# Two filter taps per slot until the second pair's keys, and second-layer scores one slot after the first transposes

## The chip, the cores and the metric

The kernel runs on one core of a Trainium2 chip. Its engines run side by side, each through its own list of instructions in order: TensorE (PE, matmuls), VectorE (DVE), ScalarE (ACT), GpSimd (POOL) and SyncE (SP, which issues most DMAs). The metric is the device time of one execution in microseconds.

## The reference

Two layers run over 256 latent tokens, which layer 1 extends by 256 context tokens. Each layer projects the normalised tokens to a convolution branch, queries, keys and values of eight attention heads, and gates; both branches are joined by the gates and projected out, and a gated MLP follows. Cut to what bears on the change:

```python
p = h @ w_in[l]
u = a * jax.nn.sigmoid(g)                  # convolution branch, 512 channels
u = dwconv1d(u, dw, dw_b)                  # 31 taps along the tokens
u = jax.nn.silu(layernorm(u, ln_g, ln_b)) @ w_conv_out
q, k = rope_2d(q, ...), rope_2d(k, ...)
s = concat([s_window + bias, s_context])   # neighbourhood window and all context keys
y_attn = merge_heads(softmax(s) @ v) @ w_na_out
x = x + g1 * ((g_conv * y_conv + g_attn * y_attn) @ w_out)
x = x + g2 * conv_ffn(h2, w_up, dw, dw_b, w_down)
```

All is float32.

## The kernel before, in words

Tokens lie along the free dimension: 512 columns in the first layer (`self.l` or `l` is 0), 256 in the second (`last`), where only the keys and values still have context columns. Weights come as units of 128 x 1024, loaded by SP. Every float32 product is three matmuls (`mm3`, L187 to L189): high part of the weights by high and low part of the tokens, low part of the weights by the high part of the tokens. ACT casts the high part of a unit (L168 or L206); the low part is a subtraction on DVE (L169), or, for some units, a negation on ACT (L207) and an accumulating DMA that POOL issues (L208). The names in a trace are `whi` and `wlo` for these, `h` for the tokens' parts, `raw` for a unit as loaded.

A *group* is eight such products into one PSUM bank, 24 matmuls. After each group of 256 columns, and twice in a group of 512, `slot()` lets every side generator go one step. The side generators spread other work between the groups:

- `conv_run` (the convolution) takes `rate[0]` taps per slot from a list; a tap is one DVE instruction on one of four channel tiles (`cb`, L651; the first of a tile is L649).
- `Attention.run` calls `step()`. Heads go in four pairs. `qk(j)` makes a pair's queries and keys: two groups, rotary products on DVE (L839 to L849), the high part on ACT (L861), the low part on DVE (L862), and a load of the bias on SP (L837). `pair(j)` then puts the pair on `todo`, with the slot at which it came. `issue()` takes it from there: score products on PE (L472, twelve for the latent queries), which fill four PSUM banks (`sc`, `sc`, `pt`, `main`), and the softmax: bias and maximum on DVE (L493), exponential on ACT (L496), reciprocal on DVE (L498), scaling on ACT (L499). The result is `pp`. `turn()` transposes it on PE (L538) into the same four banks and copies these out on ACT (L541, for the context queries L544). `values()` makes the products with the values (L555, L564) into the bank `po`, which ACT and DVE empty (L572, L573).

`self.soft` holds softmaxes that wait to be transposed, `self.pv` transposes that wait for their values, `self.at` the number of the last step that did something. A step issues, in one go, transposes of the last pair, values of the one before it, and scores of the next. While nothing is waiting for its values yet, that is at the first transposes, `alone` makes the first layer issue the transposes by themselves; `late` then has the next scores issued at the next slot.

After the attention and the gates (`gate`, L693 and L696) comes the layer norm of the convolution, again as a side generator: it takes the taps that are left, five or six a slot, sums on PE (L939, L354), spreads the reciprocal root (L369), and writes the result's parts `sh` and `sl` (L950 to L954). Then PE runs the attention's projection (U_NA, on `oh` and `ol`), the convolution's (U_CO, on `sh` and `sl`), where DVE joins the branches (L977, L982 to L985), and the output projection.

A scheduler puts the instructions of this program into a list per engine, by priorities and modelled times; `issue_after` binds some to a place. So an edit of when something is issued can move rows on every engine.

Of the kernel before, what the change touches and what calls it, by code (L numbers as in the profile page):

```python
# [53 lines left out]
def trunk(ctx: ExitStack, tc: tile.TileContext, xt, cvec, crow, wall, wada, params, bias_t, rope_t, out):  # L54
# [13 lines left out]
    def nm(s):  # L68
        uid[0] += 1
        return f"{s}_{uid[0]}"  # L70
# [3 lines left out]
    def psum(tag="main"):  # L74
        return psp.tile([P, 512], F32, tag=tag, bufs=BANKS[tag], name=nm(tag))

    def tmp(w=512):
        return tp.tile([P, w], F32, tag="t", bufs=5, name=nm("t"))
# [10 lines left out]
    def add_side(gen):  # L89
        side.append(gen)  # L90
# [87 lines left out]
    def wunit(l, u, at=None, cuts=1):  # L178
        w, more = wparts(l, u, at, cuts)
        more()  # L180
        return w
# [221 lines left out]
    class Attention:  # L403
# [33 lines left out]
        def step(self, now=False):  # L437
            self.n += 1
            since = self.n - self.at
            alone = not self.l and self.soft and not self.pv and not self.late  # L440
            if not now and since < (4 if self.todo or alone else 3 if self.soft else 2) and not self.late:
                return
            if not now and not alone and not self.todo and self.pairs < 4:
                return
            if not now and not alone and self.todo and self.n - self.todo[0][0] < 2:
                return
            if self.late:
                self.late, self.at = False, self.n
                return self.issue()
            if alone and not now:  # L450
                self.late = True
            self.at = self.n
            pv, self.pv = self.pv, []
            soft, self.soft = self.soft, []
            for what, its, pps in soft:
                with tc.issue_after(self.last.ins), tc.issue_after(self.done.ins):
                    self.turn(what, its, pps)
            for work in pv:
                self.values(*work, "sc" if work[0] == CTX and not (soft or self.todo) else "po")
            if self.todo and not self.late:  # L460
                self.issue()
# [113 lines left out]
    def blocks(ap):  # L575
        return ap.rearrange("p (r b c) -> p b r c", r=ROWS, b=NB_)
# [33 lines left out]
    for l in range(DEPTH):  # L610
        last = l == DEPTH - 1
# [4 lines left out]
        with ExitStack() if last else start as e1a:  # L616
# [36 lines left out]
            rate = [0.0]  # L653

            def conv_run():
                due = 0.0
                while True:
                    due += rate[0]
                    while due >= 1:
                        due -= 1  # L660
                        if taps:
                            conv_tap(*taps.pop(0))
                    yield
# [13 lines left out]
            def in_group(t, c, tag="main"):  # L677
                return group(psum(tag), unit8(l, U_IN + t), *h1, c)

            def glu_groups(j):  # L680
                pa = in_group(T_GLU + 2 * (j - 1), ALL)
                pg = in_group(T_GLU + 2 * (j - 1) + 1, ALL)
                copied = None if last else att.ahead(j - 2)
                with tc.issue_after(copied.ins) if copied else ExitStack():
                    glu(j, pa, pg)
# [12 lines left out]
            with ExitStack() as e1b:  # L698
# [5 lines left out]
                def keep_v(t, ps):  # L704
                    if t > 1:
                        act.copy(V[t - 2], ps)
                        return
                    v = tmp()
                    act.copy(v, ps)
                    for b in range(NB_):  # L710
                        for r in range(2):
                            at = r * GW + BASE[b]
                            sp.dma_start(VW[2 * t + r :: ROWS, b], v[at : at + WC])  # L713

                def v_tile(pv, w, k, toks, parts=range(3)):
                    i = k % 2
                    for t in toks:
                        c = slice(t * P, (t + 1) * P)
                        b = slice(i * 512, (i + 1) * 512)
                        for n in parts:  # L720
                            mm = pe.matmul(  # L721
                                pv[t], h1[n == 1][k][:, c], w[n == 2][:, b], start=k + n == 0, stop=k == KD - 1 and n == 2
                            )
                    return mm
# [95 lines left out]
                    glu_groups(1)  # L820

                conv = conv_run()
                rate[0] = 3 if last else 3.0
                add_side(conv)

                def qk(j):

                    att.ahead(j - 2)
                    bt = eb.tile([P, 5, NS_ // 2], F32, tag="bias", bufs=2 if last else 1, name=nm("bias"))
                    both = []  # L830
                    for what in range(2):
                        w = T if what == 0 else 2 * S
                        sc = HD ** -0.5 if what == 0 else 1.0
                        ps = in_group((T_Q, T_K)[what] + j, slice(0, w))
                        if what == 0:
                            with tc.issue_after(lastdma[0].ins):
                                sp.dma_start(bt, bias_t[l, j])  # L837
                        r1, r2 = tmp(), tmp()
                        dve.tensor_tensor(r1[:, LAT], ps[:, LAT], rope[:, 0, :], ALU.mult)  # L839
                        dve.stream_shuffle(r2[:, LAT], ps[:, LAT], SWAP16)  # L840
                        dve.tensor_tensor(r2[:, LAT], r2[:, LAT], rope[:, 1, :], ALU.mult)
                        if what == 0:
                            rq = tmp()
                            dve.tensor_tensor(
                                rq[:, LAT].rearrange("p (b r c) -> p b r c", b=NB_, r=ROWS),
                                blocks(r1[:, LAT]), blocks(r2[:, LAT]), ALU.add,
                            )
                        else:
                            dve.tensor_tensor(r1[:, LAT], r1[:, LAT], r2[:, LAT], ALU.add)  # L849
                        f = eb.tile([P, 2, KN if what else w], F32R, tag="qk"[what], bufs=2, name=nm("qk"))  # L850
                        if what == 0:
                            to = [([f[:, a, LAT] for a in range(2)], rq[:, LAT])]
                            if T > S:
                                to.append(([f[:, a, CTX] for a in range(2)], ps[:, CTX]))
                        else:
                            rv_ = r1[:, LAT].rearrange("p (r c) -> p r c", r=ROWS)
                            to = [([f[:, a, KCTX] for a in range(2)], ps[:, CTX])]
                            for d, c in ((slice(0, KL), slice(GW - TC, GW)), (slice(KX, KN), slice(0, TC))):
                                to.append(([f[:, a, d].rearrange("p (c r) -> p r c", r=ROWS) for a in range(2)], rv_[:, :, c]))
                        for (hi, lo), src in to:  # L860
                            act.activation(hi, src, AF.Identity, scale=sc)  # L861
                            end = dve.scalar_tensor_tensor(lo, src, sc, hi.bitcast(F32), ALU.mult, ALU.subtract)  # L862
                        both.append(f)
                    att.pair(j, *both, bt, end)

                if l == 0:
                    for t in range(4):
                        keep_v(t, pv[t])
                    qk(0)
                    arun = att.run()  # L870
                    add_side(arun)
                    for j in range(1, 4):
                        glu_groups(j)
                        qk(j)
                else:
                    wvs = [wunit(l, U_V + uu) for uu in range(4)]
                    for half in range(2):
                        pv = {t: psum() for t in (2 * half, 2 * half + 1)}
                        for k in range(KD):
                            v_tile(pv, wvs[k // 2], k, pv)  # L880
                            if k % 2:
                                slot()
                        for t, p in pv.items():
                            keep_v(t, p)
                    glu_groups(2)
                    rate[0] = 3
                    qk(0)
                    glu_groups(3)
                    arun = att.run()
# [439 lines left out]
```

## Time and profile before

| | us |
|---|---|
| runs | 1121.14, 1121.38, 1122.13 (median 1121.38) |
| the profiled execution, its own time | 1121.24 |
| its span, first to last instruction | 1119.4 |
| PE busy | 1104.5 |
| DVE busy | 887.7 |
| ACT busy | 582.5 |
| mean granted clock of PE | 0.995 of full speed |

The span is what the trace covers; 1.8 us of the execution lie around it. In a row of the timeline the columns are the start and the busy time in us, the engine, the line, the operation, its tiles with out and in, their shapes, the count, and in brackets the idle time of the engine before the row with what ended it. Matmuls overlap, so the distance between two starts, not the busy time, is what one adds. In a row of a stretch the columns are its bounds, its length, each engine's busy time with its instructions, the clock of PE, and the share and rate of the DMA engines.

### The profile page before, as it was taken

The page shows a single profiled execution, that of the slowest core. Times are in us where ns is not written, and L with a number is a line of the kernel's source. Part 1 is how long each engine was busy: PE and PEld are TensorE (multiplying, and loading weights), DVE is VectorE, ACT ScalarE, POOL GpSimd, SP SyncE. Part 2 cuts the span into 40 slices and gives each one's busy share as a digit, 9 for nine tenths or more (in the row PEclk, how much of TensorE's full clock was granted, in tenths as well). Part 3 has the DMA queues.
Part 4 walks back from the last instruction along what each step waited for, and adds up shares of the span by engine and source line. Part 5 has one row for each costly group of instructions (what it writes and reads, how often), then busy time and mean ns, then how long its engine had stood idle before and what let it go on. Part 6 is the DMA issues. An engine that isn't in the chain of part 4 may idle for free.

```text
span 1119.4 us, 18216 instructions
## 1 busy us (share of the span) xinstructions
PE 1104.5 (99%) x6990; PEld 956.0 (85%) x6990; DVE 887.7 (79%) x1615; ACT 582.5 (52%) x968; POOL 36.2 (3%) x50
## 2 busy tenths in 40 slices
PE   9999999999999999999999999999999999999997
PEld 7777777787789988888888888989899999999997
DVE  5579899875878788887898555789699898988773
ACT  4458878541333543434333223544778667666642
POOL 1011110000000000000000000000100000000000
PEclk9999999999999999999999999999999999999999
DMA  9988562645743354554556655567864474665781
GB/s 367 288 205 209 147 171 68 195 160 165 250 133 124 116 157 150 169 168 152 167 172 211 214 191 192 175 202 198 230 172 145 154 251 164 192 199 176 220 269 58
DMA packets 59223, 205.60 MB, mean 184 GB/s; under 512 B 7168, under 2 KB 7424, under 8 KB 59136
## 3 DMA queue, kind: packets, MB, share of 16 engines
q1 hardware_dynamic: 55104, 190.77, 53.0%
q0 software_dynamic: 3744, 13.63, 6.4%
q8 instruction: 55, 0.90, 0.3%
q14 instruction: 32, 0.26, 0.1%
q10 hardware_dynamic: 288, 0.04, 0.0%
HBM read 187.63 MB, written 1.05 MB: 169 GB/s over the span
## 4 chain that ended last, share of the span: by engine, by line
PE 88%; DVE 5%; ACT 4%; SPq 1%; issue 1%; DMA 1%; DVEq 0%; ACTq 0%
PE main L187 25%; PE main L189 25%; PE main L188 25%; PE main L721 4%; DVE cb L651 2%; SPq L713 1%; PE sc L187 1%; PE sc L189 1%; PE sc L188 1%; PE po L220 1%; PE po L555 1%; ACT whi L206 1%; ACT whi L168 1%; DVE wlo L169 0%; ACT wlo L207 0%
## 5 line engine op out<-in xcount | busy, mean ns | idle before, releaser
L187 PE MATMUL main<-h,whi 128*128 128x256 f32 (+1 forms) x1328 | 448.0, 338 | 0.0
L189 PE MATMUL main<-h,wlo 128*128 128x256 f32 (+1 forms) x1328 | 444.4, 336 | 1.0 <-DVE wlo L169 1.0
L188 PE MATMUL main<-h,whi 128*128 128x256 f32 (+1 forms) x1328 | 443.8, 335 | 0.1
L168 ACT CAST whi<-raw 128x1024 fp32r<-128x1024 f32 (+1 forms) x218 | 225.5, 1038 | 256.4 <-DMA raw<-in_wall 124.0
L169 DVE TENSOR_TENSOR wlo<-raw,whi 128x1024 fp32r<-128x1024 f32 (+1 forms) x218 | 261.9, 1207 | 99.7 <-ACT whi L168 97.8
L187 PEld LDWEIGHTS main<-h,whi 128*128 128x128 f32 x1328 | 250.6, 189 | 30.8 <-issue 2.6
L189 PEld LDWEIGHTS main<-h,wlo 128*128 128x128 f32 x1328 | 250.5, 189 | 29.7 <-DVE wlo L169 1.5
L188 PEld LDWEIGHTS main<-h,whi 128*128 128x128 f32 x1328 | 250.9, 189 | 28.7 <-DVE h L385 0.5
L651 DVE SCALAR_TENSOR_TENSOR cb<-u,par,cb 128x512 f32<-128x512 f32 (+1 forms) x240 | 144.5, 615 | 3.0
L289 DVE CUSTOM_DVE_ANT_0 t<-raw,sb,par 128x1024 bf16<-128x1024 f32 x100 | 126.6, 1278 | 2.1 <-DMA raw<-in_wada 2.1
L187 PE MATMUL main<-fh,whi 128*128 128x256 f32 (+1 forms) x386 | 123.0, 319 | 0.0
L188 PE MATMUL main<-fl,whi 128*128 128x256 f32 (+1 forms) x386 | 123.0, 319 | 0.0
L189 PE MATMUL main<-fh,wlo 128*128 128x256 f32 (+1 forms) x386 | 122.9, 318 | 0.0
L188 PEld LDWEIGHTS main<-fl,whi 128*128 128x128 f32 x386 | 72.7, 188 | 5.6
L189 PEld LDWEIGHTS main<-fh,wlo 128*128 128x128 f32 x386 | 72.7, 188 | 5.6
L187 PEld LDWEIGHTS main<-fh,whi 128*128 128x128 f32 x386 | 72.7, 188 | 5.5
L1055 ACT ACTIVATE t<-main,par 128x512 f32<-128x512 f32 (+1 forms) x82 | 50.6, 667 | 36.6 <-PE main L189 36.6
L1056 DVE SCALAR_TENSOR_TENSOR t<-main,par,t 128x510 f32<-128x510 f32 (+1 forms) x82 | 47.5, 615 | 9.0 <-ACT t L1055 8.7
L1059 DVE SCALAR_TENSOR_TENSOR t<-main,par,t 128x510 f32<-128x510 f32 (+1 forms) x82 | 46.6, 610 | 0.0
L384 ACT ACTIVATE h<-t,mod 128x256 fp32r<-128x256 f32 x56 | 25.4, 502 | 37.2 <-DVE t L383 37.2
L721 PE MATMUL main<-whi,h 128*128 128x512 f32 x128 | 40.5, 401 | 0.1
L990 DVE SCALAR_TENSOR_TENSOR x<-main,mod,x 128x256 f32<-128x256 f32 x48 | 22.1, 479 | 22.8 <-PE main L189 22.7
(224 smaller groups left out, 1249.2 us busy)
## 6 DMA issues: line engine op xcount, KB each, us to landing
raw<-in_wall SPq DMA_DIRECT2D x239, 512.0 KB, 4.3
raw<-in_wada SPq DMA_DIRECT2D x88, 512.0 KB, 4.5
wlo<-raw POOLq DMA_DIRECT2D x26, 512.0 KB, 5.3
bias<-in_bias_t SPq DMA_DIRECT2D x8, 520.0 KB, 5.2
row<-in_wada SPq DMA_DIRECT2D x8, 512.0 KB, 4.7
sb<-in_crow SPq DMA_DIRECT2D x5, 512.0 KB, 5.6
x<-in_xt SPq DMA_DIRECT2D x8, 256.0 KB, 4.2
raw<-in_wall SPq DMA_DIRECT2D x8, 256.0 KB, 6.9
```

Of the source, the lines that this page charges most:

```text
L168: act.copy(hi[:, c], r[:, c])
L169: dve.tensor_tensor(lo[:, c], r[:, c], hi[:, c].bitcast(F32), ALU.subtract)
L187: pe.matmul(ps, w[0], xh, start=start, stop=False)
L188: pe.matmul(ps, w[0], xl, start=False, stop=False)
L189: pe.matmul(ps, w[1], xh, start=False, stop=stop)
L289: dve.tensor_tensor_reduce(tmp().bitcast(BF16), r, v, 1.0, pr(l, BADA + n, 1), ALU.mult, ALU.add, mods[l][:, n, s : s + 1])
L384: high = act.activation(hi[:, c], y[:, c], AF.Identity, bias=b)
L651: dve.scalar_tensor_tensor(cb[j], src, w, cb[j], ALU.mult, ALU.add)
L721: mm = pe.matmul(pv[t], h1[n == 1][k][:, c], w[n == 2][:, b], start=k + n == 0, stop=k == KD - 1 and n == 2)
L1055: act.activation(c, pv_, AF.Identity, bias=pr(l, FDB + t, 1), scale=w[1])
L1056: dve.scalar_tensor_tensor(c[:, :, 1:], pv_[:, :, : S - 1], w[0], c[:, :, 1:], ALU.mult, ALU.add)
L1059: dve.scalar_tensor_tensor(c[:, :, : S - 1], pv_[:, :, 1:], w[2], c[:, :, : S - 1], ALU.mult, ALU.add)
```

## The change

Three edits. In the first layer `rate[0]` is 2 in place of 3 from the start of the convolution until the second pair's keys have been issued (the first turn of the loop over `j`), and 3 from then on. In the second layer the first transposes are issued alone too, as in the first. And the late scores are issued at the first slot at which a pair stands on `todo` since two slots or more, in place of the next slot whatever stands there.

```diff
@@ -437,7 +437,7 @@
         def step(self, now=False):
             self.n += 1
             since = self.n - self.at
-            alone = not self.l and self.soft and not self.pv and not self.late
+            alone = self.soft and not self.pv and not self.late
@@ -445,6 +445,8 @@
             if not now and not alone and self.todo and self.n - self.todo[0][0] < 2:
                 return
             if self.late:
+                if not self.todo or self.n - self.todo[0][0] < 2:
+                    return
                 self.late, self.at = False, self.n
                 return self.issue()
@@ -820,7 +822,7 @@
                 conv = conv_run()
-                rate[0] = 3 if last else 3.0
+                rate[0] = 3 if last else 2.0
                 add_side(conv)
@@ -872,6 +874,7 @@
                     for j in range(1, 4):
                         glu_groups(j)
                         qk(j)
+                        rate[0] = 3
```

In what follows the lines of the changed kernel are numbered two higher from L447 on and three higher from L877 on (a tap is L653, score products L474, the low part of the keys L864).

DVE in the first layer, at the second pair's keys (`main_967`, `main_957` after, is the bank of the key group; `t` are the rotary products, `qk` the keys' parts, `cb` the taps). Before:

```order
L651 SCALAR_TENSOR_TENSOR cb_0_199<-u_0_212,par,cb_0_199 128x512
L651 SCALAR_TENSOR_TENSOR cb_1_200<-u_1_213,par,cb_1_200 128x512
L839 TENSOR_TENSOR t_1038<-main_967,rope_211 128x256
L651 SCALAR_TENSOR_TENSOR cb_1_200<-u_1_213,par,cb_1_200 128x512
L840 STREAM_SHUFFLE t_1039<-main_967 128x256
L651 SCALAR_TENSOR_TENSOR cb_1_200<-u_1_213,par,cb_1_200 128x512
L841 TENSOR_TENSOR t_1039<-t_1039,rope_211 128x256
L651 SCALAR_TENSOR_TENSOR cb_1_200<-u_1_213,par,cb_1_200 128x512
L849 TENSOR_TENSOR t_1038<-t_1038,t_1039 128x256
L862 SCALAR_TENSOR_TENSOR qk_1044<-main_967,qk_1044 128x256
L651 SCALAR_TENSOR_TENSOR cb_1_200<-u_1_213,par,cb_1_200 128x512
L862 SCALAR_TENSOR_TENSOR qk_1044<-t_1038,qk_1044 128x4x40 x2
```

The same place after:

```order
L653 SCALAR_TENSOR_TENSOR cb_0_199<-u_0_212,par,cb_0_199 128x512
L841 TENSOR_TENSOR t_1026<-main_957,rope_211 128x256
L842 STREAM_SHUFFLE t_1027<-main_957 128x256
L653 SCALAR_TENSOR_TENSOR cb_0_199<-u_0_212,par,cb_0_199 128x512
L843 TENSOR_TENSOR t_1027<-t_1027,rope_211 128x256
L864 SCALAR_TENSOR_TENSOR qk_1032<-main_957,qk_1032 128x256
L851 TENSOR_TENSOR t_1026<-t_1026,t_1027 128x256
L653 SCALAR_TENSOR_TENSOR cb_0_199<-u_0_212,par,cb_0_199 128x512 x2
L864 SCALAR_TENSOR_TENSOR qk_1032<-t_1026,qk_1032 128x4x40 x2
```

Between the first rotary product and its sum (L849, then L851) stands one tap instead of three, and the context keys' low part stands ahead of the sum; two taps follow it instead of one.

PE in the second layer, behind the transposes of the first pair (`ident` is the identity they multiply by; `h` and `whi` make a gate group). Before, the next scores stand right behind them:

```order
L538 MATMUL pt_7545<-ident,pp_7388 128x64
L538 MATMUL main_7546<-ident,pp_7388 128x64
L472 MATMUL sc_7561<-qk_7400,qk_7306 128x416
L472 MATMUL sc_7562<-qk_7400,qk_7306 128x416
...
L472 MATMUL main_7570<-qk_7400,qk_7306 128x416
L187 MATMUL main_7622<-h_5569,whi_7625 128x256
L188 MATMUL main_7622<-h_5577,whi_7625 128x256
```

After:

```order
L540 MATMUL pt_7545<-ident,pp_7388 128x64
L540 MATMUL main_7546<-ident,pp_7388 128x64
L187 MATMUL main_7574<-h_5569,whi_7577 128x256
L188 MATMUL main_7574<-h_5577,whi_7577 128x256
...
L189 MATMUL main_7574<-h_5576,wlo_7578 128x256
L474 MATMUL sc_7609<-qk_7400,qk_7306 128x416
L474 MATMUL sc_7610<-qk_7400,qk_7306 128x416
```

A whole gate group, 24 matmuls, has moved ahead of the scores; the later steps of the attention stand one such group later too.

PE in the second layer, where U_CO begins (row 4612 of PE's list in both kernels). Before:

```order
L187 MATMUL main_8721<-sh_0_8352,whi_8716 128x256
L188 MATMUL main_8721<-sl_0_8356,whi_8716 128x256
L189 MATMUL main_8721<-sh_0_8352,wlo_8717 128x256
L187 MATMUL main_8721<-sh_1_8353,whi_8716 128x256
L187 MATMUL main_8739<-sh_0_8352,whi_8716 128x256
```

After:

```order
L187 MATMUL main_8722<-sh_0_8389,whi_8717 128x256
L187 MATMUL main_8740<-sh_0_8389,whi_8717 128x256
L187 MATMUL main_8764<-sh_0_8389,whi_8759 128x256
L188 MATMUL main_8722<-sl_0_8393,whi_8717 128x256
L189 MATMUL main_8722<-sh_0_8389,wlo_8718 128x256
```

The matmuls on `sh` are drawn ahead, so that the first on `sl` is the fourth and not the second; the first on the last tile's `sl` is the 41st instead of the 35th. The layer norm's matmuls stand 12 rows later: its sum L939 was row 4525 and is row 4537, its L369 was row 4575 and is row 4587.

## The prediction

> **What bounds the kernel now.** I read the shares and the chain of work on the page first, then TensorE's (PE's) waits, then the stretches around the waits that the change touches, then each engine's rows there.
>
> ```profile
> PE 1104.5 (99%) x6990; PEld 956.0 (85%) x6990; DVE 887.7 (79%) x1615; ACT 582.5 (52%) x968; POOL 36.2 (3%) x50
> PE 88%; DVE 5%; ACT 4%; SPq 1%; issue 1%; DMA 1%; DVEq 0%; ACTq 0%
> ```
>
> PE is the bound: the change issues the same matmuls, so it can only win PE's idle time and time at a lowered clock. The waits of PE (engine, line, releaser: total us, times, longest):
>
> ```profile
> PE main L189 <- DVE wlo L169: 1.7, 3, 0.6
> PE sc L472 <- ACT qk L861: 1.2, 1, 1.2
> PE sc L472 <- ACT pT L544: 0.8, 1, 0.8
> ...
> PE pt L472 <- ACT pT L541: 0.6, 1, 0.6
> ...
> PE sc L472 <- DVE qk L862: 0.5, 1, 0.5
> PE sc L472 <- ACT pT L541: 0.4, 1, 0.4
> ```
>
> Five stand ahead of score products (L472). Their places on PE:
>
> ```profile
> 102.43 0.46 PE L472 MATMUL sc<-qk,qk 64*128 64x416 f32 x2 [1.19 <-ACT qk L861]
> 103.34 0.64 PE L472 MATMUL sc<-qk,qk 64*128 64x416 f32 x4 [0.46 <-DVE qk L862]
> 111.82 0.59 PE L538 MATMUL sc<-ident,pp 64*128 64x64 f32 x12
> 136.22 1.14 PE L472 MATMUL sc<-qk,qk 64*128 64x416 f32 x5 [0.76 <-ACT pT L544]
> 808.57 1.21 PE L472 MATMUL sc<-qk,qk 64*128 64x416 f32 x6 [0.39 <-ACT pT L541]
> 810.41 0.45 PE L472 MATMUL pt<-qk,qk 64*128 64x416 f32 x1 [0.63 <-ACT pT L541]
> ```
>
> In layer 1 the second pair's scores wait 1.19 + 0.46 = 1.65 us for their keys; in layer 2 they wait 0.39 + 0.63 = 1.02 us for copies that empty the banks. The stretches there (us; busy time and count by engine; PE clock; DMA):
>
> ```profile
> 105.00:110.00 5.00, 5.00 (x16) 3.91 (x16) 5.00 (x16) 3.41 (x9) 0.59 (x1) 0.67 0.83 209
> 135.00:140.00 5.00, 4.21 (x36) 3.16 (x33) 5.00 (x11) 2.90 (x6) 0.86 (x1) 1.00 0.90 252
> 810.00:815.00 5.00, 4.59 (x25) 4.32 (x26) 4.68 (x17) 5.00 (x14) 0.86 (x1) 0.66 0.64 173
> ```
>
> Right after both waits the granted clock falls: (1 - 0.67) x 5 = 1.7 us are lost at 105, (1 - 0.66) x 5 = 1.7 at 810. The 0.76 us before 136.22 cost no clock (1.00). So, as I read it, about 1 us of idle time close together lowers the clock for a stretch, and each pair of waits costs its own length and 1.7 more.
>
> [...]
>
> **The change, layer 1: two taps per slot until the second pair's keys.** VectorE (DVE) is what the keys wait for:
>
> ```profile
> 88.93 0.16 DVE L498 RECIPROCAL ri<-sm 128x1 f32<-128x1 f32 x1 [1.54 <-ACT pp L496]
> ...
> 92.15 0.42 DVE L839 TENSOR_TENSOR t<-main,rope 128x256 f32<-128x256 f32 x1
> 98.15 0.41 DVE L839 TENSOR_TENSOR t<-main,rope 128x256 f32<-128x256 f32 x1
> 98.49 0.73 DVE L651 SCALAR_TENSOR_TENSOR cb<-u,par,cb 128x512 f32<-128x512 f32 x1
> 101.48 0.41 DVE L862 SCALAR_TENSOR_TENSOR qk<-main,qk 128x256 fp32r<-128x256 f32 x1
> 102.48 0.81 DVE L862 SCALAR_TENSOR_TENSOR qk<-t,qk 128x160 fp32r<-128x160 f32 x2
> 103.20 2.32 DVE L651 SCALAR_TENSOR_TENSOR cb<-u,par,cb 128x512 f32<-128x512 f32 x3
> ```
>
> A tap takes 0.66 us (98.49 to the next instruction), a rope step or low part 0.34. The runs of taps shorten a lot earlier on, but DVE then waits 1.54 us for ScalarE's (ACT's) first exponentials at 88.93 anyway, so only what lies behind that counts. There, by the order, five taps instead of six stand between the query rope (92.15) and the key rope (98.15), one instead of three between that and the sum L849; the context low part (L862 at 101.48, 0.34) moves ahead of L849, and the two taps after L849 stand ahead of the last low part. The start loses 0.2 (a whole tap in place of the shorter first tap). Key rope: 98.15 + 0.2 - 0.66 = 97.7. L849 ends four steps of 0.34, one tap and one 0.34 low part later: 100.0; ACT's high part, behind a weight cast, 101.25; the low part 100.0 + 1.32 + 0.72 = 102.1. ACT and PE meet there so:
>
> ```profile
> 101.60 0.78 ACT L861 ACTIVATE qk<-t 128x160 fp32r<-128x160 f32 x2 [1.58 <-DVE t L849]
> 106.11 0.61 ACT L496 ACTIVATE pp<-sc,mx 128x416 f32<-128x416 f32 x1 [1.79 <-DVE mx L493]
> 107.29 0.61 ACT L496 ACTIVATE pp<-sc,mx 128x416 f32<-128x416 f32 x1 [0.48 <-DVE mx L493]
> 110.24 1.17 ACT L499 ACTIVATE pp<-pp,ri 128x416 f32<-128x416 f32 x2
> 111.69 1.05 ACT L206 CAST whi<-raw 128x1024 fp32r<-128x1024 f32 x1 [0.28 <-PE main L188]
> ```
>
> PE is free at 102.43 - 1.19 = 101.24, so the 1.19 goes; the two first products then wait about 0.45 for the low part. Idle 1.65 becomes 0.45: -1.2 us; and 0.45 is under the 0.76 that cost no clock: -1.7 us. PE is 2.9 us earlier.
>
> What is late next is ACT. The transposes L538 (111.82) would start at 108.9, but their last input, the second of the L499, ended at 111.41. DVE is through with the low part at 102.1 instead of 103.2, and three taps stand behind it in both orders, so the maxima and ACT's exponentials start 1.1 to 1.2 earlier; the taps between the maxima go, which takes out the 0.48 us that ACT idled between its first two exponentials (107.29). ACT ends near 111.4 - 1.7 = 109.7, and the last six transposes, due at 109.6, wait 0.1 (0 if ACT gains 2 us, 0.7 if only the 1.1). Then the context scores need ACT's copies, which stand behind the cast L206 (1.05): +0.5, from 0 to the 0.63 that such a wait took at 810. At 136 PE has moved some 2.3 us, ACT by what DVE lets it: +0.1, bounded by 0.5 either way. The withheld taps are given out later, in front of the layer norm; on PE that norm moves nine triplets back, and its users in the next projection stand some 170 matmuls behind it, over 40 us at 0.23: free. The bias load goes out one weight unit earlier on SP's queue, and pushes that unit back by one load; the weight casts here wait for PE or DVE in the rows above, not for a load: free. Layer 1: -1.2 - 1.7 + 0.1 + 0.5 + 0.1 = **-2.2 us** (-3.4 to 0.5).
>
> **The change, layer 2: transposes alone, a gate group, then the scores.** The group is 24 matmuls of 256 at 0.118, 2.8 us; the copies, late by 1.02 at most, are done within it: -1.02. Without that idle time the clock stays: -1.7. Moved past the group is everything that attention does from there on. The group's and the next units' low parts must now come sooner: one goes out at 806.69 and takes up to 8.1 us,
>
> ```profile
> 806.69 0.88 POOL L208 DMA_DIRECT2D wlo<-raw  x1 [1.44 <-ACT wlo L207]
> DMA to landing us min/median/max: 6.2/7.2/8.1
> ```
>
> so it may land at 812.9 to 814.8. It belongs to the query group behind the moved scores: 807.23 + 0.95 (24 transposes) + 2.8 + 1.4 (12 scores) + 0.1 = 812.5, plus the two high-part matmuls ahead of it. I take 0.1, from 0 to 2.0.
>
> The price is at the end. Every attention step is a gate group later, so the layer norm's matmuls stand 12 rows (1.4 us) closer to the projection U_CO, which reads its result:
>
> ```profile
> 820.00:865.00 45.00, 45.00 (x456) 41.31 (x455) 42.71 (x93) 34.41 (x77) 1.58 (x1) 1.00 0.47 144
> 881.50 0.47 DVE L950 SCALAR_TENSOR_TENSOR cb<-cb,par,po 128x256 f32<-128x256 f32 x1
> 885.55 0.28 PE L187 MATMUL main<-sh,whi 128*128 128x256 f32 x1
> 888.97 0.42 DVE L954 TENSOR_TENSOR sl<-cb,sh 128x256 fp32r<-128x256 f32 x1
> 897.07 1.22 DVE L169 TENSOR_TENSOR wlo<-raw,whi 128x1024 fp32r<-128x1024 f32 x1
> ```
>
> Before, the last low part (888.97 + 0.42 = 889.4) meets its matmul, the 35th of U_CO, at 885.55 + 34 x 0.117 = 889.5: no slack. The matmul becomes the 41st (4.7 us after U_CO's start), the norm's broadcast ends 2.6 us ahead of that start instead of 4.0, and 7.8 us of DVE work (881.50 to 889.4, in which a second low-part subtraction of 1.14 now stands) brings it at 5.2 to 6.3 us. Wait 0.5 to 1.6; I take 1.0, as DVE has slack of only 0.4 to take up the subtraction. The same subtraction for the output projection (897.07), for which PE now waits up to 0.6, is ordered one 0.34 step later: +0.35 (0 to 0.8). Layer 2: -1.02 - 1.7 + 0.1 + 1.0 + 0.35 = **-1.3 us** (-2.4 to 2.4).
>
> **Sum.** -2.2 - 1.3 = -3.5 on the profiled execution's own 1121.24 us (span 1119.4, 1.8 around it), 0.14 under the median 1121.38: **1117.7 us**.
>
> **Rivals.** (A) One lowered stretch stays, at the new waits: 0.45 at 102, 0.1 and 0.5 from 109 to 113 or 0.9 at 136 in layer 1, 1.0 and 0.35 in layer 2; 1.02 was enough at 810, 0.76 was not at 136: 1117.7 + 1.7 = 1119.4. [...] (C) Layer 1's taps move nothing, because ACT's weight casts release the keys: its 2.2 are not gained, 1119.9. Against it: L861 itself waited 1.58 us for DVE. (D) Slower: DVE can't come forward. From 820 to 865 it is busy 42.71 of 45. If it gains nothing, the last low part comes at 889.4 + 1.4 + 1.14 = 891.9, and is wanted at 885.55 - 2.7 + 4.7 = 887.5: a wait of 4.4 us, long enough for two lowered stretches (3.4). Layer 2 is then -2.7 + 4.4 + 3.4 + 0.35 = 5.5, and the time 1121.24 - 2.2 + 5.5 = 1124.5. It decides from a wait of 3.5 on. Against it: DVE idled 2.3 us in that window and could use it.
>
> **How the numbers follow.** Chances: forecast 0.47, A 0.24, B 0.06, C 0.10, D 0.13. The range takes the forecast's lower end (copies and norm wait for nothing) and D's lower half: 1115.8 to 1122.0; the forecast alone holds 1115.8 to 1119.1. About 0.2% (2.2 us) can be told from no change here, so faster means under 1119.1. The forecast lies there, with 0.10 of A and 0.02 of C: faster 0.59; the rest of A, B and C, and 0.02 of D: 0.30; slower 0.11.
>
> **What the new profile would show.** Right: waits of the second pair's scores under 0.5 in both layers; clock 1.00 at 105 and 810; new short waits of L538 and the context scores near 110; waits for sl (L954's new line) at U_CO. Wrong: 0.67 anywhere else after 100, a wait for a wlo landing by DMA at 812, or waits over 2 us ahead of U_CO.

## The result and the profile after

| | before | changed |
|---|---|---|
| median of 21 runs, us | 1120.94 | 1123.69 |
| lowest to highest | 1119.83 to 1124.14 | 1121.07 to 1131.30 |
| span of the profiled execution | 1119.4 | 1122.5 |

The changed kernel takes 1.0034 times as long (95% interval 1.0024 to 1.0043; this ratio on record is not the quotient of the medians, which would be 1.0025). It is slower by some 3 us, where 1117.7 us and a gain had been forecast, and lies outside the range of 1115.8 to 1122.0. Its times also spread more.

The page of the changed kernel, in the rows that answer to those shown of before:

```profile
PE 1104.8 (98%) x6990; PEld 956.0 (85%) x6990; DVE 886.3 (79%) x1615; ACT 583.4 (52%) x969; POOL 36.3 (3%) x50
PE 82%; DVE 9%; ACT 5%; issue 3%; DMA 1%; SPq 1%; POOL 0%; DVEq 0%; ACTq 0%; POOLq 0%
```

The work is the same; PE's part of the chain falls from 88% to 82%, DVE's rises from 5% to 9%. DMA reads 1% in both, but 9.40 us of it are now the landing of a low part, at 806.18, which was not in the chain before. PE's waits in the changed kernel (line and releaser, total us, times, longest):

```profile
PE main L189 <- DMA wlo<-raw: 3.2, 1, 3.2
PE main L189 <- DVE wlo L169: 1.8, 3, 0.7
...
PE sc L474 <- ACT pT L546: 1.1, 1, 1.1
PE po L942 <- DVE ss L939: 0.8, 1, 0.8
...
PE main L187 <- ACT whi L168: 0.4, 1, 0.4
PE pt L540 <- ACT pp L519: 0.2, 1, 0.2
PE pt L474 <- ACT pT L543: 0.2, 1, 0.2
PE main L188 <- DVE sl L957: 0.2, 1, 0.2
```

Of the five waits ahead of scores that the change is about, the two for the second pair's keys (1.2 and 0.5) and the two of the second layer (0.4 and 0.6) are gone; the fifth is 1.1 in place of 0.8. In their place stand 3.2 us for a landing and 0.8 for the sum of the first layer's norm, neither of which was there before. The stretches that answer to those of before:

```profile
105.00:110.00 5.00, 5.00 (x44) 3.86 (x44) 4.76 (x13) 5.00 (x13) 0.00 (x0) 1.00 0.98 252
810.00:815.00 5.00, 2.44 (x20) 1.82 (x19) 4.77 (x14) 4.70 (x11) 0.86 (x1) 1.00 0.92 234
815.00:820.00 5.00, 4.37 (x23) 4.38 (x24) 1.82 (x7) 2.46 (x7) 0.00 (x0) 0.66 0.86 202
```

The clock stays at 1.00 at 105 (0.67 before) and at 810 (0.66 before). But at 810 PE is busy half the time (2.44 of 5.00 us), and behind that, at 815, the clock is 0.66.

The rows on PE, in order of time:

```profile
101.15 1.16 PE L474 MATMUL sc<-qk,qk 64*128 64x416 f32 x6
108.59 0.59 PE L540 MATMUL sc<-ident,pp 64*128 64x64 f32 x12
133.88 1.32 PE L474 MATMUL sc<-qk,qk 64*128 64x416 f32 x6 [1.11 <-ACT pT L546]
187.45 0.27 PE L540 MATMUL pt<-ident,pp 64*128 64x64 f32 x1 [0.24 <-ACT pp L519]
214.46 1.09 PE L942 MATMUL po<-ss,one 128*128 128x512 f32 x2 [0.83 <-DVE ss L939]
806.69 0.59 PE L540 MATMUL sc<-ident,pp 64*128 64x64 f32 x12
810.62 0.83 PE L474 MATMUL sc<-qk,qk 64*128 64x416 f32 x6
815.63 0.38 PE L189 MATMUL main<-h,wlo 128*128 128x256 f32 x1 [3.18 <-DMA wlo<-raw]
887.01 0.52 PE L187 MATMUL main<-sh,whi 128*128 128x256 f32 x3
892.50 0.39 PE L188 MATMUL main<-sl,whi 128*128 128x256 f32 x1 [0.17 <-DVE sl L957]
900.58 0.37 PE L187 MATMUL main<-h,whi 128*128 128x256 f32 x1 [0.37 <-ACT whi L168]
901.62 0.39 PE L189 MATMUL main<-h,wlo 128*128 128x256 f32 x1 [0.56 <-DVE wlo L169]
934.02 0.38 PE L369 MATMUL po<-ident,rs 128*128 128x128 f32 x2
```

Set beside the same instructions of before, these starts give the account. A minus means ahead of before. The whole change and each half alone (the first two experiments) have a column, and so has a second profile of the kernel before.

| start of | before | changed | taps alone | late scores alone | before again |
|---|---|---|---|---|---|
| second pair's transposes | 111.82 | -3.23 | -2.20 | -1.22 | +0.86 |
| third pair's scores | 136.22 | -2.34 | -1.32 | -0.05 | +0.84 |
| products behind the last context transposes (L555) | 189.74 | -1.56 | -0.56 | -0.08 | +0.84 |
| attention's projection U_NA, layer 1 | 261.19 | -0.50 | +1.00 | -0.07 | +1.08 |
| first transposes, layer 2 | 807.23 | -0.54 | +1.00 | -0.02 | +1.13 |
| U_NA, layer 2 | 873.01 | +1.46 | -0.52 | +1.09 | -0.39 |
| U_CO, layer 2 | 885.55 | +1.46 | -0.53 | +1.09 | -0.38 |
| broadcast of the MLP's norm, layer 2 (L369) | 931.02 | +3.00 | -0.53 | +4.43 | +0.30 |

So in this pair of profiles layer 1 first gains what was forecast (2.34 at 136, forecast 2.2), and gives 1.8 of it back at 188 and 214. Layer 2 loses 2.0 until U_NA and 1.5 behind U_CO. The last column shows how far two profiles of one kernel lie apart, 1.5 us between 807 and U_NA above all, where the clock fell in the first of them alone (0.66 at 810, 1.00 in the second).

### The profile page after: what moved, and what is told of

Read it like the earlier page. It is cut to its first block, busy times and chain, and to the rows that moved or that the text cites. A ratio compares the mean times of both kernels' runs of the same rounds, so it can differ in the third digit from the quotient of the medians.

```text
span 1122.5 us, 18220 instructions
## 1 busy us (share of the span) xinstructions
PE 1104.8 (98%) x6990; PEld 956.0 (85%) x6990; DVE 886.3 (79%) x1615; ACT 583.4 (52%) x969; POOL 36.3 (3%) x50
## 3 DMA queue, kind: packets, MB, share of 16 engines
HBM read 187.63 MB, written 1.05 MB: 168 GB/s over the span
## 4 chain that ended last, share of the span: by engine, by line
PE 82%; DVE 9%; ACT 5%; issue 3%; DMA 1%; SPq 1%; POOL 0%; DVEq 0%; ACTq 0%; POOLq 0%
PE main L187 24%; PE main L189 24%; PE main L188 23%; DVE cb L653 4%; PE main L723 4%; DVE wlo L169 1%; PE sc L187 1%; PE sc L189 1%; PE sc L188 1%; DMA wlo<-raw 1%; PE po L220 1%; SPq L715 1%; PE sc L137 1%; ACT wlo L207 1%; DMA raw<-in_wall 1%
## 5 line engine op out<-in xcount | busy, mean ns | idle before, releaser
L653 DVE SCALAR_TENSOR_TENSOR cb<-u,par,cb 128x512 f32<-128x512 f32 (+1 forms) x240 | 143.7, 614 | 2.7
```

The source lines that it names most:

```text
L653: dve.scalar_tensor_tensor(cb[j], src, w, cb[j], ALU.mult, ALU.add)
```

## The experiments

All times are medians with the kernel before's on the same chip beside them.

**The taps edit alone, and the second layer's edits alone.** The first is the third and fourth hunk of the diff, the other the first and second.

> The taps edit alone, on the kernel before. Theory 1 (the withheld taps come back): the second pair's scores no longer wait, the clock stays up at 105, and TensorE is 2.3 us ahead at 136, but the taps given out later make it wait about 0.8 at the last context transposes near 188 and 0.8 to 1.0 for the layer norm's sum near 214, so 0.5 us is left: about 1120.4 against 1120.9. Rival 1 (the two waits of the changed kernel near 188 and 214 are chance, and not the taps'): they are absent, 2.3 us are left: about 1118.6.

> The edits of the second layer alone, on the kernel before. Theory 2 (the low part that comes by DMA is late): TensorE comes to the third query group about 3 us sooner than before and waits there for a low part that takes 6 to 9.5 us to land after its issue near 806.5; wait 0 to 4 us, with a lowered clock where it is over 1: 1121 to 1126, with a wide spread, median about 1123.5. Rival 2 (the layer norm's lateness makes the loss, by waits at the convolution's projection and at the output projection): no wait for a landing, waits for sl and wlo of 2 us or more near 890 to 902, about 1122 with the small spread of before.

Measured: taps alone 1121.33 against 1120.47, ratio 1.0006 (0.9995 to 1.0016); late scores alone 1122.39, ratio 1.0018 (1.0006 to 1.0030). Neither half gains; together they come near the whole. With the taps alone, on PE:

```profile
188.45 0.27 PE L538 MATMUL pt<-ident,pp 64*128 64x64 f32 x1 [0.23 <-ACT pp L517]
215.95 0.67 PE L940 MATMUL po<-ss,one 128*128 128x512 f32 x1 [1.03 <-DVE ss L937]
```

Both later waits are there, so they are the taps' doing, and more than the gain is lost: -1.34 ahead of 188 becomes +1.00 at U_NA. Theory 1 holds, with a loss larger than it said. With the late scores alone, the waits:

```profile
PE main L189 <- DVE wlo L169: 3.4, 4, 1.5
PE main L189 <- DMA wlo<-raw: 2.3, 1, 2.3
```

Both theory 2 and its rival are right in part: 2.3 us for the landing (and a clock of 0.68 behind it), and 3.3 us between U_CO and the MLP's norm.

**The third query unit's low part on VectorE.** `ADDED` lists the units whose low part comes by the accumulating DMA; in the changed kernel, unit 9 of the second layer is taken out.

```diff
-ADDED = {*((0, U_IN + i) for i in range(19)), *((1, U_IN + i) for i in (7, 8, 9, 14, 15, 16, 17))}
+ADDED = {*((0, U_IN + i) for i in range(19)), *((1, U_IN + i) for i in (7, 8, 14, 15, 16, 17))}
```

> The changed kernel, but the low part of the third query unit of the second layer is subtracted on VectorE and not accumulated by a DMA. Theory 2: the wait of 3.2 us and the lowered clock behind it go, at the price of 1.14 us on VectorE that is partly hidden: 1118.5 to 1120, and the spread of the times is as small as before's. Rival 2: the time stays within 1 us of the changed kernel's 1123.7.

Measured: 1122.88 against 1120.47, ratio 1.0018 (1.0009 to 1.0027). In the profile the wait for the landing and the lowered clock behind it are gone (mean clock 0.998, 0.996 in the changed kernel's), and U_NA is 1.9 us further ahead than the first transposes (-0.99 after +0.93). But then 3.4 us are lost between U_CO and L369 (+2.38), so theory 2 names only one of two losses, and the median stays within the rival's 1 us of the changed kernel's, though the ratio to the kernel before falls from 1.0034 to 1.0018. The long executions are gone, as theory 2 said: none of 11 over 1124.3, where 8 of the changed kernel's 21 were, on another occasion.

**The first layer's norm two slots later behind its sums,** in the changed kernel.

```diff
-                    yield
+                    for _ in range(1 if last else 3):
+                        yield
                     pm = psum("po")
```

> The changed kernel with the first layer's layer norm two slots later behind its sums (its matmul L942 stands one group later on TensorE). Theory 1: the wait of 0.83 us for the sum near 214 goes, nothing else in layer 1 moves since its result is used 40 us later: layer 1 gains 1 us, about 1122.7 against 1123.7 (hidden partly by the spread of that kernel; the profile decides). Rival 1: a wait of the same length stands elsewhere, no gain.

Measured: 1122.57 against 1120.47, ratio 1.0014 (1.0005 to 1.0022), 1.1 under the changed kernel's median, measured on another occasion. The wait for the sum is gone: U_NA of layer 1 at -0.25, after -0.48 at 190. But 0.9 is lost again in layer 1's output projection, where a new wait of 0.42 stands:

```profile
317.93 0.50 PE L188 MATMUL main<-h,whi 128*128 128x512 f32 x1 [0.42 <-DVE h L989]
```

So the norm's sum can be taken later, but not for nothing.

**The second layer's norm, sooner in the changed kernel and later in the kernel before.** The two edits of one line:

```diff
-                    for _ in range(2 if last else 4):
+                    for _ in range(1 if last else 4):
```

```diff
-                    for _ in range(2 if last else 4):
+                    for _ in range(3 if last else 4):
```

> The changed kernel with the second layer's layer norm one slot sooner behind its squares (its broadcast 32 rows ahead of the convolution's projection U_CO on TensorE; 25 in the changed kernel, 37 before). Theory 3 (the norm's lateness puts the low parts of the first output units behind the joins on VectorE, their raw buffers come free later, and the next weights come late): the offset to the kernel before no longer grows between U_CO and the MLP's norm, where it grew by 1.5 to 3.4 us in the four kernels with the late norm; the time falls by about as much, to 1121 or 1122 from 1123.7 beside 1120.5 before. Rival 3 (the growth comes from where the attention leaves VectorE, not from the norm's place): it grows as much as before.

> The kernel before with nothing changed but the second layer's layer norm one slot later behind its squares, which puts its broadcast 25 rows ahead of U_CO, exactly where it stands in the changed kernel. Theory 3: the loss of 1.5 to 3.4 us between U_CO and the MLP's norm is there without the rest of the change: 1122 to 1124 against 1120.5. Rival 3: no loss, 1120.5.

Measured: sooner 1120.90 against 1120.49, ratio 1.0003 (0.9994 to 1.0012), and all runs between 1120.0 and 1121.7; later, in the kernel before, 1122.27, ratio 1.0012 (1.0002 to 1.0021). The second changes nothing else, and its PE rows show the loss by itself:

```profile
884.04 0.52 PE L187 MATMUL main<-sh,whi 128*128 128x256 f32 x3
897.14 0.36 PE L187 MATMUL main<-h,whi 128*128 128x256 f32 x1 [0.38 <-ACT whi L168]
898.18 0.39 PE L189 MATMUL main<-h,wlo 128*128 128x256 f32 x1 [0.57 <-DVE wlo L169]
923.17 0.39 PE L189 MATMUL main<-h,wlo 128*128 128x258 f32 x1 [1.68 <-DVE wlo L169]
932.51 0.39 PE L369 MATMUL po<-ident,rs 128*128 128x128 f32 x2
```

From U_CO to L369 it takes 932.51 - 884.04 = 48.5 us where before took 931.02 - 885.55 = 45.5. The loss has three places, by the starts of the same rows counted from U_CO's start: 0.4 at the rows on `sl`, 0.7 at 897 and 898, 1.9 at 923. In the changed kernel they are 0.9, 0.7 (at 900 and 901) and nothing: its whole 1.5 is lost before 902. The way to the third, as it begins in the changed kernel: DVE's subtraction of an output unit, the next load on SP's queue, ACT's cast of it:

```profile
900.36 1.21 DVE L169 TENSOR_TENSOR wlo<-raw,whi 128x1024 fp32r<-128x1024 f32 x1
...
901.95 0.33 SPq L165 DMA_DIRECT2D raw<-in_wall  x1
...
905.66 1.05 ACT L168 CAST whi<-raw 128x1024 fp32r<-128x1024 f32 x1 [2.98 <-DMA raw<-in_wall]
```

A late norm pushes the subtraction (897.07 before, 900.36 now, while PE is only 1.46 later) behind the joins on DVE, and PE waits for it at 901.62. The raw buffer that it reads is free only then, the next load goes out at 901.95 (898.36 before, by SP's rows), and ACT waits 2.98 for it. In the changed kernel's profile this second delay costs PE nothing. In the kernel with the late norm ACT still waits at 916, ahead of PE's wait at 923:

```profile
916.83 1.05 ACT L168 CAST whi<-raw 128x1024 fp32r<-128x1024 f32 x1 [3.07 <-DMA raw<-in_wall]
```

Of six profiles with the late norm three have such a third wait (1.5 to 1.7), one loses 0.3 there and two nothing; what decides is open. That the buffers carry the delay that far is read from the rows and was not tried by itself.

With the norm one slot sooner the growth was 1.06, not none: U_CO loses 0.8 at `sl` all the same, and 0.35 go at L369 to a wait for POOL's `rs`, where the kernel before's second profile loses 0.6 too. The loss at the output units is gone. So theory 3 holds, by the edit that moves the norm alone. The time of the sooner norm came out as expected, but by luck in the main: in its profile the landing was no wait, and U_NA came at -2.22, +1.46 in the changed kernel.

**Both remedies without the taps.** The second layer's edits, the query unit's low part on VectorE, the norm one slot sooner.

> The second layer's edits alone, with the third query unit's low part subtracted on VectorE and the layer norm one slot sooner; no taps edit. If theories 2 and 3 name the whole loss of the second layer, the gain of the late scores is left: their waits of 1.0 us and, in the executions in which the clock falls there, 1.7 more: 1118.5 to 1120 against 1120.5. If something else in these edits costs as much, 1120.5 or more.

Measured: 1120.69 against 1120.49, ratio 1.0001 (0.9992 to 1.0010). Nothing is gained, which is what had been expected if something else costs as much. The profile names it: with the low part on VectorE a wait of 0.7 for the emptied banks is back (as in the two other kernels that have it there), and from U_CO to L369 1.25 are still lost (U_CO -1.22, L369 +0.03).

**The kernel before, and the changed one, for a second profile.** No edit.

> The kernel before once more, for a second profile. [...]

> The changed kernel once more, for a second profile. Theory 2: the wait for the third query unit's low part is another than 3.2 us (0 to 4), as its landing differs between executions; the waits near 188, at the norm's sum (0.8 to 1.0) and at the first output units (0.4 and 0.6) are the same. Rival 2b: 3.2 us again.

The kernel before's second execution, 1121.60 us, first the waits, then the two stretches:

```profile
PE sc L472 <- ACT qk L861: 1.6, 1, 1.6
...
PE pt L472 <- ACT pT L541: 0.6, 1, 0.6
...
PE sc L472 <- DVE qk L862: 0.4, 1, 0.4
...
PE sc L472 <- ACT pT L541: 0.4, 1, 0.4
```

```profile
105.00:110.00 5.00, 5.00 (x19) 3.70 (x16) 4.96 (x15) 2.73 (x8) 0.86 (x1) 0.67 0.93 233
810.00:815.00 5.00, 4.38 (x34) 3.67 (x34) 4.65 (x17) 4.31 (x13) 0.86 (x1) 1.00 0.72 177
```

The same waits, and the clock fell behind the first (0.67) and not behind the second (1.00). (The span, 1119.8, is not shorter than the 1119.4 of the first execution for that: PE was already 1.1 us behind at 807, 0.4 of it by the longer key wait.) So the clock falls behind the same waits in some executions only; what decides in which, no run shows. Of eight profiles with the key waits of before, the clock fell behind them in three (0.67, 0.67 and 0.71 at 105, 1.00 in the other five); of five with the second layer's waits of before, in one, the one that the prediction read (0.66 at 810, 1.00 in the other four).

What a fall is worth can be read too. In the kernel with the late norm the key waits were 1.5 and 0.5, and this stretch and this row followed:

```profile
105.00:110.00 5.00, 5.00 (x22) 4.07 (x23) 4.96 (x15) 2.96 (x8) 0.86 (x1) 1.00 0.95 221
114.92 0.38 PE L472 MATMUL pt<-qk,qk 64*128 64x256 f32 x1 [0.23 <-ACT pT L541]
```

PE began the second pair's scores 0.45 later than in the profile of before and, at full clock, their transposes 1.12 sooner. But ACT's copies of these stood where they had stood (112.69 and 114.39; before 112.65 and 114.34), PE waited for ACT, and the third pair's scores came at 136.27, where they had come at 136.22. The five profiles with the key waits of before and a clock of 1.00 at 105 gain 0.4 from 102 to 136 on the one that the prediction read, not 1.7. In layer 2 nothing takes the gain back: in the four profiles with before's order and a clock of 1.00 at 810, U_NA comes 1.5 sooner behind the first transposes than in that one.

The changed kernel's second execution took 1125.97 us, and waited 2.3 for the landing, not 3.2; the sum's wait was 1.0, those at the output units 0.4 and 0.6. Theory 2 as expected.

**Making up for the taps, and keeping the norm's rows.** In the first layer `rate[0] = 4 if j < 3 else 3` behind `qk(j)` in place of `rate[0] = 3`; in the second, where the norm takes the taps that are left:

```diff
-                        for _ in range(6 if last else 5):
+                        for _ in range(8 if last else 5):
```

The first alone with the taps edit; the other alone with the late scores; and all together.

> The taps edit alone, but with four taps per slot, not three, from the second pair's keys to the fourth's, so that the withheld taps are made up for before the layer norm, whose sum stands 12 rows sooner on TensorE than before. Theory 1: the waits near 188 and for the norm's sum go, and 1 to 2 us of the gain at the second pair's keys are left: 1119 to 1119.8 against 1120.5. Rival 1b (VectorE has no room for them sooner, so the later keys wait in their place): the waits ahead of the scores at 136 and 163 grow, 1120.5 or more.

> The second layer's edits alone (no taps edit), with up to eight instead of six of the left taps per slot in the second layer's layer norm, which puts all its matmuls back on the rows that they have in the kernel before. Theory 3: no growth of more than 0.5 us between U_CO and the MLP's norm; the time is that of the kernel before less the two waits of 1.0 us and a part of the clock, plus what a late landing costs in some executions: 1119 to 1121 against 1120.5. Rival 3: the growth of 1.5 to 3.4 us stays, 1122 or more.

> Both halves of the change with both remedies: four taps per slot after the second pair's keys, eight of the left taps per slot in the second layer's norm. If the losses named by theories 1 and 3 are all of them but a late landing, 1118 to 1120 against 1120.5; if the layers' losses come back elsewhere, 1120.5 or more.

Four taps: 1122.16 against 1120.39, ratio 1.0013 (1.0004 to 1.0023). The sum's wait is gone but 0.7 of waits came at the second pair's transposes, and 0.8 stand at the third pair's scores, in two pieces. Against before, PE is 0.83 ahead at 136, level at 160 and 1.3 behind at 190: the last context transposes lose more than without the remedy. This is rival 1b at the scores, and theory 1 holds for the sum alone. Eight taps with the late scores: 1119.74, ratio 0.9999 (0.9984 to 1.0013); the profile has U_CO at -2.93 and L369 at -2.91, no growth, as theory 3 said. From the first transposes to U_NA it gains 2.6 on the profile of before, 1.05 more than before's order at full clock: the 1.02 of waits that the prediction wanted. All together: 1121.71, ratio 1.0012 (1.0003 to 1.0022); its profile loses 1.2 us in layer 1 and no more in layer 2's norm, so the taps edit costs more than it brings with this remedy too.

**The landing, by itself.** The late scores with eight taps, once with the low part on VectorE and once more as it was:

> The second layer's edits with eight of the left taps per slot in the norm, and the third query unit's low part subtracted on VectorE. Theory 2 (its late landing makes the long executions): no execution over 1123, median 1119 to 1120. Rival: as many long executions as with the DMA, so the spread has another cause.

> The same with the low part by DMA as in the run before, on the same chip as its pair: the median 0.5 to 1 us under the kernel before's, some executions 2 to 7 us over the median (theory 2); with the rival no more of these than in its pair.

Measured: on VectorE 1119.11 (1118.75 to 1120.62) against 1120.50, ratio 0.9993 (0.9984 to 1.0003); by DMA 1119.21 (1118.60 to 1121.86), ratio 0.9995 (0.9986 to 1.0005). No execution of the pair was long, so it doesn't tell what the long ones are made of; the first time, one of twelve with the DMA took 1127. These are the best versions found, 1.3 to 1.4 us under before by the medians; the intervals still include no change.

## Why the prediction was wrong, step by step

**Key waits, -1.2.** About right: -1.28 in the changed kernel's profile, -0.7 to -0.8 in four others with the same taps, -1.43 in one. The low part came without a wait in one and with 0.5 to 0.6 in others, and in two ACT's high part kept a wait of 0.3 to 0.4.

**The clock, -1.7 twice.** This is the largest term, and it was mis-sized. One execution was read as the kernel. The clock does fall behind such waits, but in 3 of 8 profiles (to 0.67 and 0.71) and in 1 of 5 (to 0.66), and of the 1.7 at 105 only 0.4 is left at 136, where PE otherwise waits for ACT: 0.4 x 3/8 + 1.5 x 1/5 = 0.45 us is an estimate of what these falls cost on average, not 3.4. The kernel before's median on more runs, 1120.4 to 1120.9, lies under the profiled 1121.24, and of its 112 executions beside the experiments only 16 had a mean clock of 0.995 or less, as the profiled one had. The prediction did not ask whether the same wait has a lowered clock behind it in every execution. The clock fell behind waits of 1.65 us in sum, and once behind 1.02, and stayed at 1.00 behind 1.6 (1.2 and 0.4, late scores with eight taps) and behind 1.0 (0.4 and 0.6, the kernel before's second profile).

**New waits near 110, +0.6, and +0.1 at 136.** Measured: 0.2 for the copies, and 1.1 for the third pair's scores in place of 0.8. Right in size. The sum at 136 came out at -2.34 in the changed kernel's profile, but at -1.2 to -2.0 in five others with the same taps: that it met the forecast 2.2 is in part luck.

**"Free", at the first layer's norm.** This is the step that failed in layer 1. It looked only at who uses the norm's result. But the sum L939 is itself a row in PE's list, and everything behind it waits for DVE's last taps: 0.8 to 1.0 us of wait, 1.1 to 1.6 lost (2.0 in one profile with another wait of 0.5 ahead of it). The other 0.8, near 188, comes from ACT's order:

```profile
185.07 1.28 ACT L908 ACT_TABLE_LOAD   x1
186.37 0.63 ACT L908 ACTIVATE g<-g 128x512 f32<-128x512 f32 x1
186.90 0.89 ACT L519 ACTIVATE pp<-pp,ri 128x256 f32<-128x256 f32 x2
```

In the changed kernel a table load and a gate's sigmoid stand ahead of the last two scalings, on which the transposes wait; before, they stood behind. The change's order on ACT was not read there.

**The low part's landing, +0.1 (0 to 2.0).** This is the step that failed in layer 2, and the dearest of all. The place, the need at 812.4 and the issue near 806 were right (812.45 and 806.18). But the landing took 9.4 us, against 6.2 to 8.1 for two such DMAs in the one profile (6.2 for this one), and made 3.2 of wait and 1.7 of clock. The prediction had named this wait, and a lowered clock at another place, as signs of its being wrong; both came. The wait was 3.2, 2.3, 2.3, 0.6, 0.2 and three times none in the eight profiles with this order. The range held the wait of most of them but left out the clock behind it. A gain that brings PE 3 us sooner to a transfer is paid out only as far as the transfer allows.

**The norm's lateness, +1.0 and +0.35.** About right in the profiled pair. The last low part came 5.4 us after U_CO's start (892.03 + 0.41), at the early end of the reckoning, and its matmul 0.70 later than the same row of before, counted from that start. U_CO lost 0.9 in all; the idle time of 0.2 on the page shows only part of it, as the two matmuls that waited started 0.42 and 0.44 behind their forerunners in place of 0.12. The output units lost 0.7. What the two terms left out is the third wait, through the raw buffers: with it the loss was 3.0 to 3.4 in three of six profiles, 1.5 to 1.8 in the others. Rival D's wait of 4.4 for `sl`, with two lowered stretches, did not come; that it is long enough for two was an estimate, which no run shows (behind the 3.2 for the landing came one, 0.66 at 815). That its 1124.5 lies beside the profiled 1124.24 is luck.

**Sum.** For the profiled pair: forecast -2.2 - 1.3 = -3.5; measured -0.5 in layer 1, +2.0 to U_NA and +1.5 behind U_CO in layer 2, together +3.0. The landing with its clock (3.2 + 1.7 in place of 0.1) and the 1.8 in layer 1 that had been put at nothing account for this difference of 6.5. For the medians the clock term comes on top, as most executions of the kernel before have no fall to lose.

## What to carry to other kernels

A lowered clock in one profile belongs to that execution until a second profile shows it again: take it into the sum with the share of executions that have it (here 3 of 8 and 1 of 5 profiles), and only as far as the engine wouldn't wait for another one in its place (here 0.4 of 1.7 us). When work is withheld from a full engine and given out later, follow it to the in-order row of the bounding engine that waits for its last piece, whoever uses the result (here L939, 0.8 to 1.0 us of wait). When an order table moves a side task by one group, look at its buffers: in the kernel with the late norm PE waited 0.57 for a late subtraction at 898, and 1.68 for another at 923, 25 us later; between them ACT waited 3.07 for a load whose buffer, by the rows, came free late.

## What the runs showed of the hardware

Waits of 1.5 and 0.5 us on PE, 0.5 us apart, passed at a clock of 1.00 (the kernel with the late norm, from 100 to 110), and behind waits of 0.39 and 0.63 it was 0.66 in one execution (the kernel before's first profile, from 810 to 815): length alone does not decide.

The accumulating DMA of the third query unit took longer the closer the loads ahead of it were: 9.4 us at 1.15 us behind the weight load, 5.9 at 2.64. Rows of the changed kernel, and of the late scores with eight taps:

```profile
805.03 0.33 SPq L165 DMA_DIRECT2D raw<-in_wall  x1
805.41 0.42 SPq L839 DMA_DIRECT2D bias<-in_bias_t  x1
806.18 0.88 POOL L208 DMA_DIRECT2D wlo<-raw  x1 [1.45 <-ACT wlo L207]
DMA to landing us min/median/max: 5.5/7.4/9.4
```

```profile
803.73 0.33 SPq L165 DMA_DIRECT2D raw<-in_wall  x1
804.11 0.42 SPq L839 DMA_DIRECT2D bias<-in_bias_t  x1
806.37 0.88 POOL L208 DMA_DIRECT2D wlo<-raw  x1 [1.43 <-ACT wlo L207]
DMA to landing us min/median/max: 5.7/5.8/5.9
```

The last row of each covers two such DMAs; of this one, with the bias load between it and the weight load, it is the 9.4 in the first and the 5.9 in the second. The other profiles lie in line: at 1.16 and 1.20 us the wait was 2.3, at 1.75 0.6, at 2.24 0.2, at 2.62 and 2.80 none. It is a correlation over eight executions of kernels with the late scores; the interval itself was not set in a run, and in the profile of before this DMA took 6.2 at 2.39 us, in its second 6.4 at 3.11. What makes it differ between executions of one order, and why all four profiles with the norm moved sooner had the longer interval, stays open. So does the wide spread of the changed kernel's times: it went with this DMA, but also with the norm one slot sooner. The mean clock was 0.998 in the shortest of its 21 executions and 0.995 in the two longest, which is some 3 of the 10 us between them (0.003 x 1121, an estimate).
